# Hyena filters built in the opening of a fused hybrid diffusion step, ahead of the first adaLN sums

## The chip, the cores and the metric

One Trainium2 chip, of which the kernel uses one core. The metric is the device time of one launch in microseconds. Of a core's engines the text speaks of TensorE (PE; its weight loads are PEld), VectorE (DVE), ScalarE (ACT), GpSimd (POOL) and SyncE (SP, which here only issues transfers). Each engine runs its own instructions in the order in which the program gives them to it and waits on semaphores for the others.

## The reference, cut to what matters

One layer over two groups of 128 tokens (context and latent) with a model width of 2048. Each group is normed, scaled and shifted by adaLN columns, and goes through an input projection. One branch of the token mixer is a Hyena long convolution whose filters are made by a small sine network from 128 positions:

```python
z = concat([t, cos(w * f), sin(w * f)])            # 128 x 33
h = sin(fr[0] * (z @ w1 + b1))                      # 128 x 64
h = sin(fr[1] * (h @ w2 + b2))
h = (h @ w3 + b3).reshape(L, 2, HY_ORDER, D_HY)     # 2 directions, 2 orders, 1024 channels
h = h * exp(-t * abs(decay))
k = concat([h_fwd, 0, reversed(h_bwd[1:])])
k = k / (sum(abs(k)) + FILTER_EPS)
kf = rfft(k)                                        # used as uf * kf, and then y + u * bias
...
mod = silu(c) @ w_ada + b_ada                       # shift, scale, gate, twice: 6 x 2048
h = rmsnorm(x, g_pre) * (1 + scale) + shift
proj = h @ w_in
```

The filters depend on no token and on no adaLN value; they are needed when the first projected channels go through the convolution.

## The kernel before

All weights stream once from memory in pieces of 512 KB ("halves", 256 rows by 512 columns). A half of an ordinary weight is split on arrival: ACT rounds it to a high part `wh` (L223) and DVE takes the rest `wl` (L224), and PE runs three matmuls a tile (L288 to L290). So an ordinary half is 12 matmuls of 512 columns. A half of `w_ada` is not split; PE takes it as it is (L571, a few narrow matmuls), and after eight such halves one block of shift and scale columns is done.

`run_items` (L230) goes through a list of items, one for each half, and writes out the program in that order; what it decides is decided when the program is written, not on the chip. `feed_dma` (L205) issues the loads of halves on SP's queue, with at most `R` of them not yet taken up; `feed` (L214) writes out the splits of the halves that come up to `L` items ahead. `st` (L147) holds both; it starts with L=4 and R=16, and after the eighth `w_ada` half it is set to L=5, R=8.

Side work stands in a second list, `auxq`. `push` fills it, and after each item `pop_aux` (L166) takes pieces from it: in the opening ("free") one piece after each item, `idle(us)` holding the next one back for that much planned time. A piece's instructions stand in each engine's queue where it was taken.

The opening goes as follows. Small vectors come in on ACT's queue, the constants and the token tiles `x` on SP's. A transpose gives `cT` (Silu of the conditioning vectors) and bias columns. For each group ACT squares `x` (L386), `neg2_rstd` (L359) makes the norm's factor with a Sqrt, and `spread` (L377) turns it into a row `rb` by a matmul with ones. Then the items begin: eight `w_ada` halves (`mod_block(0, 2)`), with the transposed `x` (`x_block(0)`, L408) after the first; `to_cols` (L614) and `affine` (L629) make the first modulated block `hT`; then ordinary halves of `w_in` and `w_ada` halves alternate, one `w_in`, two `w_ada`, and so on, through six blocks.

The filters are side work in this stream. `mlp1` and `mlp2` (L450, L456) are the sine network with `sin_of` (L438); `filter_loads` (L419) puts the loads of the filters' weights on SP's queue; `filt_prep` (L461) splits the decay rates; `filt_h` (L470) makes one direction of one half of the channels of one order: two matmuls `pe` whose Exp ACT takes, one float32 matmul `ph`, which DVE multiplies by the Exp, and the absolute value on DVE; `filt_n` (L496) sums the absolute values on PE (`pn`) and makes diagonals; `filt_b` (L518) spreads them (`pi`); `filt_k` (L526) is the transform of the filter (`pc`, `pb`). There are four pairs of order and channel half, so eight `filt_h` and four of each other kind. The list `filt` (L539) and the last `push` (L1475) give their order, with pauses.

Of the kernel before, what the change touches and what calls it, by code (L numbers as in the profile page):

```python
# [11 lines left out]
F32 = mybir.dt.float32  # L12
# [5 lines left out]
P = 128  # L18
D = 2048
# [81 lines left out]
def hybrid_step(ctx: ExitStack, tc: tile.TileContext, ins, y_p, y_s, st_out):  # L101
# [18 lines left out]
    def s4(shape, dt=F32, n="s4"):  # L120
        return ar.tile(shape, dt, tag="s4", name=nm(n), bufs=NS4)
# [4 lines left out]
    def aux(shape=(P, W), n="aux"):  # L126
        return ps.tile(list(shape), F32, tag="ps", name=nm(n))
# [4 lines left out]
    def small(shape, n="sml", dt=F32):  # L132
        return sm_p.tile(shape, dt, name=nm(n))
# [13 lines left out]
    st = {"dma": 0, "split": 0, "used": 0, "out": 0, "L": 4, "R": 16, "bud": 0.0, "t": 0.0, "hold": 0.0, "free": True}  # L147
# [180 lines left out]
    for g in range(2):  # L328
        for h in range(2):
            xt[g][h] = s4([P, DH], n="x")  # L330
            SP.dma_start(out=xt[g][h], in_=xsrc[g][:, h * DH:(h + 1) * DH])
    lg = small([16, 1], "lg")
# [3 lines left out]
    pv = aux((P, 64), "pv")  # L336
    PE.transpose(pv, vr, ident[:64, :64])
    cT = cp.tile([P, KD, 34], F32, name="cT")
    V.memset(cT, 0.0)
    for g in range(2):  # L340
        A.activation(cT[:, :, 2 + g], pv[:, 16 * g:16 * g + 16], AF.Silu)
    gpre = cp.tile([P, 2, KD], F32, name="gpre")
    V.tensor_copy(gpre.rearrange("p a k -> p (a k)"), pv[:, 32:64])

    pb_ = aux((P, 96), "pbco")
    PE.transpose(pb_, bco, ident[:96, :96])
    bcol = cp.tile([P, 6, KD], F32, name="bcol")
    V.tensor_copy(bcol.rearrange("p a k -> p (a k)"), pb_)
    for i in (SCALE_M, SCALE_F):
        V.tensor_scalar(out=bcol[:, i, :], in0=bcol[:, i, :], scalar1=1.0, scalar2=None, op0=ALU.add)  # L350
# [32 lines left out]
    for g in range(2):  # L383
        ssx = small([P, 2], "ss0")
        for h in range(2):
            A.activation(s4([P, DH], n="junk"), xt[g][h], AF.Square, accum_out=ssx[:, h:h + 1])  # L386
        b0 = small([P, 1], "b0")
        V.tensor_scalar(out=b0, in0=ssx[:, 0:1], scalar1=1.0 / D, scalar2=RMS_EPS, op0=ALU.mult, op1=ALU.add)
        spread(g, diag_of(neg2_rstd(ssx[:, 1:2], b0)))

    def transpose_block(src, dst, col0, by=None):

        for kk2 in range(2):
            pt = aux((P, 2, 2, P), "pt")
            for a in range(2):
                for g in range(2):
                    kk = 2 * kk2 + a
                    x = src(g)[:, col0 + kk * P:col0 + (kk + 1) * P]
                    PE.transpose(pt[:, a, g, :], x, ident)  # L399
            o, i = dst[:, 2 * kk2:2 * kk2 + 2, :], pt.rearrange("p a g t -> p a (g t)")  # L400
            if by is None:
                A.copy(o, i)
            else:
                V.tensor_tensor(out=o, in0=i, in1=by.unsqueeze(1).broadcast_to([P, 2, 2 * P]), op=ALU.mult)

    xnT = [None] * NBLK

    def x_block(j):  # L408
        def f():
            xnT[j] = s4([P, 4, 2 * P], n="xnT")  # L410
            transpose_block(lambda g: xt[g][j // 2], xnT[j], (j % 2) * W, rb)
            if j == NBLK - 1:
                xt.clear()
        return piece(0.0, f, True)
# [4 lines left out]
    def filter_loads(o):  # L419
        def f():  # L420
            if o == 0:
                fl["tsel"], fl["dec"] = s4([8, 8 * P], n="tsel"), s2("dec")[:8, :]
                SP.dma_start(out=fl["tsel"], in_=ins["tsel"])
                SP.dma_start(out=fl["dec"], in_=ins["hy_decay"][0].rearrange("d o (c n) -> (d o c) n", n=W))
                SP.dma_start(out=dftm, in_=ins["cst"][:, DFT0:CST_W])
            for d in range(2):
                q = 2 * d + o
                t = s4([FH + 1, DH], n="w3")
                SP.dma_start(out=t[0:FH, :], in_=ins["hy_w3"][0][:, q * DH:(q + 1) * DH])
                SP.dma_start(out=t[FH:FH + 1, :], in_=ins["hy_b3"][:, q * DH:(q + 1) * DH])  # L430
                fl["w3", o, d] = t
# [29 lines left out]
    def filt_prep():  # L461
        dec = fl.pop("dec")
        dech, decl, tselr = s2("dech", F32R)[:8, :], s2("decl", F32R)[:8, :], s4([8, 8 * P], F32R, "tselr")
        V.scalar_tensor_tensor(out=dec, in0=dec, scalar=-1.0, in1=dec, op0=ALU.mult, op1=ALU.max)
        V.tensor_copy(dech, dec)
        V.tensor_tensor(out=decl, in0=dec, in1=dech.bitcast(F32), op=ALU.subtract)
        V.tensor_copy(tselr, fl.pop("tsel"))
        fl["exp"] = dech, decl, tselr

    def filt_h(o, hf, d):  # L470
        def f():
            q = d * 4 + o * 2 + hf
# [4 lines left out]
            e = s2("fe")
            A.activation(e, pe_, AF.Exp)
            ph = aux(n="ph")
            PE.matmul(ph, lhsT=h2fT, rhs=fl["w3", o, d][:, hf * W:hf * W + W], start=True, stop=True)  # L480
            V.tensor_tensor(out=e, in0=ph, in1=e, op=ALU.mult)
            if d == 1:
                V.memset(e[0:1, :], 0.0)
            ab = s2("fab")
            V.scalar_tensor_tensor(out=ab, in0=e, scalar=-1.0, in1=e, op0=ALU.mult, op1=ALU.max)
            fl[o, hf, d] = (e, ab)
            if d == 1:
                h0, ab0 = fl.pop((o, hf, 0))
                V.tensor_tensor(out=ab, in0=ab, in1=ab0, op=ALU.add)
                sd = s4([P, 2, W], n="fsd")  # L490
                V.tensor_tensor(out=sd[:, 0, :], in0=h0, in1=e, op=ALU.add)
                V.tensor_tensor(out=sd[:, 1, :], in0=h0, in1=e, op=ALU.subtract)
                fl[o, hf] = sd
# [32 lines left out]
    def filt_k(o, hf):  # L526
        def f():
# [7 lines left out]
            V.tensor_tensor(out=Kre[o][:, cs], in0=Kre[o][:, cs], in1=fl["hbias", o][:, cs], op=ALU.add)  # L535
# [3 lines left out]
    filt = [[], []]  # L539
    for o in range(2):  # L540
        for hf in range(2):
            filt[o] += [piece(1.4, filt_h(o, hf, 0), True), piece(3.2, filt_h(o, hf, 1), True), idle(3.0),
                     piece(0.8, filt_n(o, hf), True), idle(2.0), piece(0.0, filt_b(o, hf), True), idle(2.0),
                     piece(2.0, filt_k(o, hf), True)]
# [925 lines left out]
    for c in range(SPLIT, NPAIR):  # L1470
# [38 lines left out]
```

## Time and profile before

| | |
|---|---|
| median of 3 runs | 1639.32 us (1638.11 to 1642.18) |
| the profiled execution's own time | 1637.93 us |
| its span, first to last instruction | 1636.2 us |
| PE busy | 1586.4 us, 97% of the span |
| DVE, ACT busy | 1192.8 us, 729.5 us |
| read from memory | 384.03 MB, 239 GB/s over the span |

The span is what the trace shows; the device time of the same execution is 1.7 us more, and the median of the runs is 1.4 us above that. PE's busy time counts a pipelined matmul to its modelled end, so an engine that is busy throughout may still run at less than its best rate.

### The profile page before, as it was taken

To read this page: it belongs to the slowest core of one execution; us is meant where nothing else is said; L and a number is where in the kernel's file an instruction comes from. 1 tells how busy PE (TensorE), PEld (TensorE's weight loads), DVE (VectorE), ACT (ScalarE), POOL (GpSimd) and SP (SyncE) were. 2 spreads that over 40 slices of the span, in tenths; PEclk is the share of its full clock that TensorE was granted. 3 is DMA by queue.
4 is the path that set the end of the run, shared out by engine and by line. 5 is a ranking of instruction groups with operands and counts; after the bars stand their busy time and mean duration, and the time that the engine had idled before them with its cause. 6 is when DMAs were issued, how large, how long until landed. Compare 5 with 4: busy or idle time off the path is not lost.

```text
span 1636.2 us, 20371 instructions
## 1 busy us (share of the span) xinstructions
PE 1586.4 (97%) x7449; PEld 1248.3 (76%) x7449; DVE 1192.8 (73%) x1659; ACT 729.5 (45%) x946; POOL 70.0 (4%) x129
## 2 busy tenths in 40 slices
PE   4999999989999999999998999999999999999997
PEld 3665677657667788888887888888888888888886
DVE  3787877777774798778997665777878667778655
ACT  4533343333334455343545555455444354555532
POOL 0000021210011100000000000000000000000000
PEclk9999999999999999999999999999999999999999
DMA  9988898998778877786865765676678856666671
GB/s 328 336 279 309 291 301 255 334 294 284 231 270 272 276 236 246 241 286 215 285 205 211 231 172 176 208 214 194 203 259 269 293 180 195 203 210 211 208 238 53
DMA packets 208476, 396.88 MB, mean 243 GB/s; under 512 B 13220, under 2 KB 29919, under 8 KB 208376
## 3 DMA queue, kind: packets, MB, share of 16 engines
q1 hardware_dynamic: 201336, 373.88, 70.5%
q0 software_dynamic: 6800, 21.62, 4.4%
q8 instruction: 58, 0.95, 0.2%
q14 instruction: 42, 0.34, 0.1%
q10 hardware_dynamic: 240, 0.08, 0.0%
HBM read 384.03 MB, written 6.30 MB: 239 GB/s over the span
## 4 chain that ended last, share of the span: by engine, by line
PE 91%; DMA 4%; DVE 2%; ACT 1%; SPq 1%; issue 0%; ACTq 0%; DVEq 0%
PE acc L288 27%; PE acc L289 27%; PE acc L290 27%; PE ada L571 3%; DMA raw<-in_w_in_dram 2%; PE put L1353 1%; DMA raw<-in_w_ada_dram 1%; DVE wl L224 1%; SPq L210 1%; DMA raw<-in_ffn_w_up_dram 1%; PE ph L480 1%; ACT wh L223 0%; PE pt L399 0%; DMA vr<-in_norm_pre_mix_dram 0%; PE po L1031 0%
## 5 line engine op out<-in xcount | busy, mean ns | idle before, releaser
L224 DVE TENSOR_TENSOR wl<-raw,wh 128x1024 fp32r<-128x1024 f32 x504 | 596.1, 1220 | 195.8 <-ACT wh L223 188.2
L223 ACT CAST wh<-raw 128x1024 fp32r<-128x1024 f32 x504 | 502.9, 1048 | 175.9 <-PE acc L289 75.5
L288 PE MATMUL acc<-wh,hTh 128*128 128x512 f32 x704 | 284.2, 404 | 6.7 <-ACT wh L223 4.1
L289 PE MATMUL acc<-wl,hTh 128*128 128x512 f32 x704 | 276.8, 393 | 4.8 <-DVE wl L224 4.8
L288 PE MATMUL acc<-wh,h2Th 128*128 128x512 f32 x704 | 278.7, 396 | 2.8 <-ACT h2Th L1256 2.8
L290 PE MATMUL acc<-wh,hTl 128*128 128x512 f32 x704 | 276.5, 393 | 0.0
L290 PE MATMUL acc<-wh,h2Tl 128*128 128x512 f32 x704 | 275.4, 391 | 0.0
L289 PE MATMUL acc<-wl,h2Th 128*128 128x512 f32 x704 | 274.4, 390 | 0.0
L288 PEld LDWEIGHTS acc<-wh,hTh 128*128 128x128 f32 x704 | 133.4, 190 | 59.0 <-ACT wh L223 15.7
L600 DVE SCALAR_TENSOR_TENSOR adac<-raw,cT,adac 128x512 f32<-128x512 f32 x240 | 164.4, 746 | 0.0
L289 PEld LDWEIGHTS acc<-wl,hTh 128*128 128x128 f32 x704 | 133.4, 190 | 33.1 <-DVE wl L224 6.4
L290 PEld LDWEIGHTS acc<-wh,hTl 128*128 128x128 f32 x704 | 133.1, 189 | 28.9 <-DVE hTl L676 0.2
L288 PEld LDWEIGHTS acc<-wh,h2Th 128*128 128x128 f32 x704 | 132.7, 188 | 29.3 <-ACT h2Th L1256 3.2
L290 PEld LDWEIGHTS acc<-wh,h2Tl 128*128 128x128 f32 x704 | 132.5, 188 | 28.8 <-DVE h2Tl L1257 0.4
L289 PEld LDWEIGHTS acc<-wl,h2Th 128*128 128x128 f32 x704 | 132.7, 189 | 26.3
L288 PE MATMUL acc<-wh,actTh 128*128 128x512 f32 x352 | 137.3, 390 | 0.0
L290 PE MATMUL acc<-wh,actTl 128*128 128x512 f32 x352 | 137.1, 389 | 0.0
L289 PE MATMUL acc<-wl,actTh 128*128 128x512 f32 x352 | 137.0, 389 | 0.0
L1358 ACT ACTIVATE uv<-put,fcw 128x256 f32<-128x256 f32 x88 | 41.7, 475 | 91.6 <-DVE uv L1361 56.1
L1339 ACT COPY u<-acc 128x512 f32<-128x512 f32 x44 | 25.8, 587 | 116.8 <-PE acc L290 115.0
L290 PEld LDWEIGHTS acc<-wh,actTl 128*128 128x128 f32 x352 | 66.1, 188 | 13.8
L289 PEld LDWEIGHTS acc<-wl,actTh 128*128 128x128 f32 x352 | 66.1, 188 | 13.7
(311 smaller groups left out, 1594.9 us busy)
## 6 DMA issues: line engine op xcount, KB each, us to landing
raw<-in_w_ada_dram SPq DMA_DIRECT2D x192, 512.0 KB, 5.8
raw<-in_w_in_dram SPq DMA_DIRECT2D x176, 512.0 KB, 5.7
raw<-in_ffn_w_up_dram SPq DMA_DIRECT2D x176, 512.0 KB, 4.2
raw<-in_ffn_w_down_dram SPq DMA_DIRECT2D x88, 512.0 KB, 5.1
raw<-in_w_out_dram SPq DMA_DIRECT2D x32, 512.0 KB, 5.1
raw<-in_w_br_hy_dram SPq DMA_DIRECT2D x16, 512.0 KB, 4.7
raw<-in_w_br_ret_dram SPq DMA_DIRECT2D x16, 512.0 KB, 5.7
shw<-in_hy_short_w_dram POOLq DMA_DIRECT2D x18, 256.0 KB, 8.9
```

Of the source, the lines that this page charges most:

```text
L210: SP.dma_start(out=h.raw.rearrange("p a n -> p (a n)").rearrange("p (a n) -> p a n", a=per), in_=h.src)
L223: A.copy(h.hi, h.raw)
L224: V.tensor_tensor(out=h.lo, in0=h.raw, in1=h.hi.bitcast(F32), op=ALU.subtract)
L288: PE.matmul(self.ps[g], lhsT=h, rhs=wh, start=first, stop=False)
L289: PE.matmul(self.ps[g], lhsT=h, rhs=wl, start=False, stop=False)
L290: PE.matmul(self.ps[g], lhsT=l, rhs=wh, start=False, stop=last)
L480: PE.matmul(ph, lhsT=h2fT, rhs=fl["w3", o, d][:, hf * W:hf * W + W], start=True, stop=True)
L571: PE.matmul(z["ps"][32 * t:32 * t + 32, :nt * P], lhsT=cT[:, kb + kk, 2 - 2 * i:34 - 2 * i], rhs=w[:, kk, :], start=i == 0 and kb + kk < 4 ...
L600: V.scalar_tensor_tensor(out=t, in0=w, scalar=c, in1=t if kt else bias, op0=ALU.mult, op1=ALU.add)
L1339: A.copy(u[:, g, :], ch.ps[g])
L1353: PE.transpose(pt[:, a, g, :], u[:, g, kk * P:(kk + 1) * P], ident)
L1358: A.activation(o, i, AF.Copy, scale=fcw[:, 1, col:col + 1])
```

## The change

The filters' loads go to the front of SP's queue, between the constants and the token tiles (`filter_loads(0)`, `x_load(0)`, `filter_loads(1)`, `x_load(1)`). The sine network, the Exp factors of all four pairs and three of the four `filt_h` are written out before the first item, around the squares and the norms. `filt_h` now does both directions in one piece, and its absolute value is on ACT. The other pieces come one after each item from the first on, without pauses. The biases are loaded later and on POOL's queue (`bias_load`), and added to `Kre` in one go (`bias_add`). The look-ahead starts with L=0, so that no `w_in` half is split before the eighth `w_ada` half is taken, and R=10.

```diff
-    st = {..., "L": 4, "R": 16, ...}
+    st = {..., "L": 0, "R": 10, ...}
...
+    filter_loads(0)
+    x_load(0)
+    filter_loads(1)
+    x_load(1)
     cT = cp.tile([P, KD, 34], F32, name="cT")
...
+    mlp1()
     gpre = cp.tile([P, 2, KD], F32, name="gpre")
...
+    filt_prep()
+    mlp2()
+    filt_e(0, 0)
+    filt_e(0, 1)
+    squares(0)
+    filt_h(0, 0)()
+    filt_e(1, 0)
+    filt_e(1, 1)
+    squares(1)
+    filt_h(0, 1)()
+    for g in range(2):
+        input_norm(g)
+    filt_h(1, 0)()
...
+    def filt_e(o, hf):
+        dech, decl, tselr = fl["exp"]
+        e = s4([P, 2, W], n="fe")
+        for d in range(2):
+            q = d * 4 + o * 2 + hf
+            pe_ = aux(n="pe")
+            PE.matmul(pe_, lhsT=tselr[:, q * P:(q + 1) * P], rhs=dech, start=True, stop=False)
+            PE.matmul(pe_, lhsT=tselr[:, q * P:(q + 1) * P], rhs=decl, start=False, stop=True)
+            A.activation(e[:, d, :], pe_, AF.Exp)
+        fl["e", o, hf] = e
+    def filt_h(o, hf):
+        def f():
+            e = fl.pop(("e", o, hf))
+            for d in range(2):
+                ph = aux(n="ph")
+                PE.matmul(ph, lhsT=h2fT, rhs=fl["w3", o, d][:, hf * W:hf * W + W], start=True, stop=True)
+                V.tensor_tensor(out=e[:, d, :], in0=ph, in1=e[:, d, :], op=ALU.mult)
+            V.memset(e[0:1, 1, :], 0.0)
+            ab, sd = s4([P, 2, W], n="fab"), s4([P, 2, W], n="fsd")
+            A.activation(ab, e, AF.Abs)
+            V.tensor_tensor(out=sd[:, 0, :], in0=e[:, 0, :], in1=e[:, 1, :], op=ALU.add)
+            V.tensor_tensor(out=sd[:, 1, :], in0=e[:, 0, :], in1=e[:, 1, :], op=ALU.subtract)
...
     def filt_n(o, hf):
         def f():
+            ab = fl.pop(("ab", o, hf))
+            V.tensor_tensor(out=ab[:, 0, :], in0=ab[:, 0, :], in1=ab[:, 1, :], op=ALU.add)
...
-            t = s4([P, DH], n="hbias")
-            SP.dma_start(out=t, in_=ins["hy_bias"][0][o].partition_broadcast(P))
+            G.dma_start(out=t, in_=ins["hy_bias"][0][o].partition_broadcast(P))
...
-    push(x_block(0), idle(3.2), mlp[0], x_block(1), idle(3.0), mlp[1], idle(2.0), piece(0.0, filter_loads(0)), x_block(2), x_block(3),
-         idle(10.0), piece(2.0, filt_prep), *filt[0], piece(0.0, filter_loads(1)), piece(0.0, filt_done(0)), idle(14.0),
-         *filt[1], piece(0.0, filt_done(1)), piece(2.0, ret_gamma),
+    push(N(0, 0), x_block(0), piece(1.0, filt_h(1, 1), True), B(0, 0), N(0, 1), K(0, 0), B(0, 1), N(1, 0), x_block(1),
+         K(0, 1), B(1, 0), N(1, 1), K(1, 0), B(1, 1), x_block(2), K(1, 1), piece(0.0, filt_done), x_block(3),
+         idle(8.0), piece(0.0, bias_load), idle(30.0), piece(2.0, ret_gamma),
          idle(4.0), piece(2.0, ret_powers), idle(4.0), piece(2.0, ret_tables), idle(6.0), piece(0.1, ret_cols, True),
+         piece(2.4, bias_add))
```

## Rows read from the trace of the kernel before

**Rows 1.** The page, busy time: engine, us, share of the span, instructions.
```profile
PE 1586.4 (97%) x7449; PEld 1248.3 (76%) x7449; DVE 1192.8 (73%) x1659; ACT 729.5 (45%) x946; POOL 70.0 (4%) x129
```

**Rows 2.** Engines by stretch: length, busy us, granted clock (PEclk), DMA share, GB/s.
```profile
8.00:16.00 8.00, 1.49 (x4) 0.86 (x4) 2.30 (x13) 5.55 (x12) 0.00 (x0) 1.00 1.05 349
30.00:34.00 4.00, 4.00 (x12) 2.89 (x11) 1.61 (x2) 1.24 (x2) 0.00 (x0) 0.66 1.09 362
180.00:200.00 20.00, 20.00 (x96) 13.56 (x96) 17.00 (x62) 5.25 (x5) 0.68 (x2) 1.00 1.01 353
```

**Rows 3.** Timeline of the opening: start, duration, engine and line, what ended its wait.
```profile
8.71 1.06 ACT L386 ACTIVATE junk<-x 128x1024 f32<-128x1024 f32 x1
...
9.26 0.25 DVE L350 TENSOR_SCALAR bcol<-bcol 128x16 f32<-128x16 f32 x2
...
10.91 1.28 ACT L362 ACT_TABLE_LOAD   x1
12.21 0.29 ACT L362 ACTIVATE nt<-ss,b 128x1 f32<-128x1 f32 x1
...
14.36 0.27 ACT L381 COPY rb<-prb 128x128 f32<-128x128 f32 x1 [1.86 <-PE prb L380]
...
19.79 1.97 PE L399 MATMUL pt<-cst,x 128*128 128x128 f32 x8
...
21.69 3.58 PE L571 MATMUL ada<-raw,cT 128*32 128x256 f32 x56
...
25.30 1.04 ACT L223 CAST wh<-raw 128x1024 fp32r<-128x1024 f32 x1 [6.15 <-DMA raw<-in_w_in_dram]
26.25 0.36 ACT L575 COPY adap<-ada 128x256 f32<-128x256 f32 x1
26.37 1.22 DVE L224 TENSOR_TENSOR wl<-raw,wh 128x1024 fp32r<-128x1024 f32 x1 [3.88 <-ACT wh L223]
...
29.04 0.62 ACT L674 CAST hTh<-xnT 128x512 fp32r<-128x512 f32 x1
...
29.71 0.79 PE L288 MATMUL acc<-wh,hTh 128*128 128x512 f32 x1 [2.61 <-ACT hTh L674]
...
34.04 0.43 PE L452 MATMUL p<-cst,hyw 33*64 33x128 f32 x2
...
34.97 1.09 PE L399 MATMUL pt<-cst,x 128*128 128x128 f32 x8
...
36.66 0.31 ACT L446 ACTIVATE h1T<-arg 64x128 f32<-64x128 f32 x1 [0.61 <-DVE arg L445]
```

**Rows 4.** The chain that ended last, 60 to 115 us: start, us, what.
```profile
62.78 0.60 DVE dec L464
...
65.19 0.50 PE pe L475
...
65.92 1.06 PE ph L480 x2
66.97 0.57 PE ada L571 x8
...
70.25 0.23 PE acc L289
...
73.34 0.98 PE pn L501 x8
...
77.89 0.86 PE pi L521 x2
...
82.70 0.86 PE pc L531 x2
```

**Rows 5.** Groups of instructions, 30 to 200 us: count, busy us, mean ns of one.
```profile
L481 DVE TENSOR_TENSOR fe<-ph,fe 128x512 f32<-128x512 f32 x8 | 5.5, 687 | 1.8 <-PE ph L480 1.8
L478 ACT ACTIVATE fe<-pe 128x512 f32<-128x512 f32 x8 | 4.8, 598 | 18.3 <-PE pe L476 18.3
...
L483 DVE MEMSET fe<- 1x512 f32 x4 | 1.9, 485 | 0.6 <-DVE fe L481 0.6
```

More of the change, by code (lines that the diff above doesn't have):

```diff
@@ L146, in hybrid_step @@
     halves, items = [], []
-    st = {"dma": 0, "split": 0, "used": 0, "out": 0, "L": 4, "R": 16, "bud": 0.0, "t": 0.0, "hold": 0.0, "free": True}
+    st = {"dma": 0, "split": 0, "used": 0, "out": 0, "L": 0, "R": 10, "bud": 0.0, "t": 0.0, "hold": 0.0, "free": True}
     def depth(look, raw):
@@ L327, in hybrid_step, with x_load @@
     xsrc = [ins["x_prompt"][0], ins["x_sample"][0]]
-    for g in range(2):
+    def x_load(g):
         for h in range(2):
@@ L333, in hybrid_step @@
     G.dma_start(out=lg, in_=ins["ret_decay_logit"][0].rearrange("d (h o) -> (d h) o", o=1))
[L336 to L350, printed above, removed]
     ones = cp.tile([P, P], F32, name="ones")
@@ L381, in spread, with squares, input_norm @@
         A.copy(rb[:, g * P:(g + 1) * P], pr)
-    for g in range(2):
-        ssx = small([P, 2], "ss0")
+    ssx0 = [small([P, 2], "ss0") for _ in range(2)]
+    def squares(g):
         for h in range(2):
-            A.activation(s4([P, DH], n="junk"), xt[g][h], AF.Square, accum_out=ssx[:, h:h + 1])
+            A.activation(s4([P, DH], n="junk"), xt[g][h], AF.Square, accum_out=ssx0[g][:, h:h + 1])
+    def input_norm(g):
         b0 = small([P, 1], "b0")
-        V.tensor_scalar(out=b0, in0=ssx[:, 0:1], scalar1=1.0 / D, scalar2=RMS_EPS, op0=ALU.mult, op1=ALU.add)
-        spread(g, diag_of(neg2_rstd(ssx[:, 1:2], b0)))
@@ L391, in transpose_block @@
[L391 to L414, printed above, removed]
+        V.tensor_scalar(out=b0, in0=ssx0[g][:, 0:1], scalar1=1.0 / D, scalar2=RMS_EPS, op0=ALU.mult, op1=ALU.add)
+        spread(g, diag_of(neg2_rstd(ssx0[g][:, 1:2], b0)))
     fl, Kre, KB = {}, {}, {}
     def filter_loads(o):
[L420 to L431, printed above, removed]
@@ new lines, in filter_loads @@
+        if o == 0:
+            fl["tsel"], fl["dec"] = s4([8, 8 * P], n="tsel"), s2("dec")[:8, :]
+            SP.dma_start(out=fl["tsel"], in_=ins["tsel"])
+            SP.dma_start(out=fl["dec"], in_=ins["hy_decay"][0].rearrange("d o (c n) -> (d o c) n", n=W))
+        for d in range(2):
+            q = 2 * d + o
+            t = s4([FH + 1, DH], n="w3")
+            SP.dma_start(out=t[0:FH, :], in_=ins["hy_w3"][0][:, q * DH:(q + 1) * DH])
+            SP.dma_start(out=t[FH:FH + 1, :], in_=ins["hy_b3"][:, q * DH:(q + 1) * DH])
+            fl["w3", o, d] = t
@@ L432, in f, with bias_load @@
+        if o == 0:
+            SP.dma_start(out=dftm, in_=ins["cst"][:, DFT0:CST_W])
+        Kre[o], KB[o] = s4([P, DH], n="Kre"), s4([P, DH], n="KB")
+    def bias_load():
+        for o in range(2):
             t = s4([P, DH], n="hbias")
-            SP.dma_start(out=t, in_=ins["hy_bias"][0][o].partition_broadcast(P))
+            G.dma_start(out=t, in_=ins["hy_bias"][0][o].partition_broadcast(P))
             fl["hbias", o] = t
-            Kre[o], KB[o] = s4([P, DH], n="Kre"), s4([P, DH], n="KB")
@@ L436, in filter_loads, with bias_add @@
-        return f
+    def bias_add():
+        for o in range(2):
+            V.tensor_tensor(out=Kre[o], in0=Kre[o], in1=fl.pop(("hbias", o)), op=ALU.add)
     def sin_of(dst, ps, b, fr):
@@ L462, in filt_prep @@
         dec = fl.pop("dec")
-        dech, decl, tselr = s2("dech", F32R)[:8, :], s2("decl", F32R)[:8, :], s4([8, 8 * P], F32R, "tselr")
+        both, tselr = s4([8, 2, W], F32R, "dech"), s4([8, 8 * P], F32R, "tselr")
+        dech, decl = both[:, 0, :], both[:, 1, :]
         V.scalar_tensor_tensor(out=dec, in0=dec, scalar=-1.0, in1=dec, op0=ALU.mult, op1=ALU.max)
@@ L468, in filt_prep @@
         fl["exp"] = dech, decl, tselr
-    def filt_h(o, hf, d):
-        def f():
+    def filt_e(o, hf):
+        dech, decl, tselr = fl["exp"]
+        e = s4([P, 2, W], n="fe")
+        for d in range(2):
             q = d * 4 + o * 2 + hf
-            dech, decl, tselr = fl["exp"]
             pe_ = aux(n="pe")
@@ L476, in f @@
             PE.matmul(pe_, lhsT=tselr[:, q * P:(q + 1) * P], rhs=decl, start=False, stop=True)
[L477 to L493, printed above, removed]
+            A.activation(e[:, d, :], pe_, AF.Exp)
[3 more added lines that the diff above has]
+            e = fl.pop(("e", o, hf))
+            for d in range(2):
+                ph = aux(n="ph")
[6 more added lines that the diff above has]
+            V.tensor_tensor(out=sd[:, 1, :], in0=e[:, 0, :], in1=e[:, 1, :], op=ALU.subtract)
+            fl[o, hf] = sd
+            fl["ab", o, hf] = ab
         return f
@@ L497, in f @@
         def f():
-            ab = fl.pop((o, hf, 1))[1]
+            ab = fl.pop(("ab", o, hf))
+            V.tensor_tensor(out=ab[:, 0, :], in0=ab[:, 0, :], in1=ab[:, 1, :], op=ALU.add)
             pn = aux((P, 4), n="pn")
             for c in range(4):
-                PE.matmul(pn[:, c:c + 1], lhsT=ab[:, c * P:(c + 1) * P], rhs=ones[:, 0:1], start=True, stop=True)
+                PE.matmul(pn[:, c:c + 1], lhsT=ab[:, 0, c * P:(c + 1) * P], rhs=ones[:, 0:1], start=True, stop=True)
             inv, dg = small([P, 4], "finv"), s2("fdg")
@@ L509, in filt_n, with filt_done @@
         return f
-    def filt_done(o):
-        def f():
+    def filt_done():
+        for o in range(2):
             for d in range(2):
                 fl.pop(("w3", o, d))
-            fl.pop(("hbias", o))
-        return f
     def filt_b(o, hf):
@@ L534, in f @@
             PE.matmul(pb, lhsT=k("S"), rhs=sd[:, 1, :], start=True, stop=True)
-            V.tensor_tensor(out=Kre[o][:, cs], in0=Kre[o][:, cs], in1=fl["hbias", o][:, cs], op=ALU.add)
             V.tensor_tensor(out=KB[o][:, cs], in0=pb, in1=inv, op=ALU.mult)
         return f
[L539 to L544, printed above, removed]
+    filter_loads(0)
@@ new lines, in hybrid_step @@
+    x_load(0)
+    filter_loads(1)
+    x_load(1)
+    cT = cp.tile([P, KD, 34], F32, name="cT")
+    V.memset(cT, 0.0)
+    pv = aux((P, 64), "pv")
+    PE.transpose(pv, vr, ident[:64, :64])
+    for g in range(2):
+        A.activation(cT[:, :, 2 + g], pv[:, 16 * g:16 * g + 16], AF.Silu)
+    mlp1()
+    gpre = cp.tile([P, 2, KD], F32, name="gpre")
+    V.tensor_copy(gpre.rearrange("p a k -> p (a k)"), pv[:, 32:64])
+    pb_ = aux((P, 96), "pbco")
+    PE.transpose(pb_, bco, ident[:96, :96])
@@ new lines, in hybrid_step, with transpose_block @@
+    bcol = cp.tile([P, 6, KD], F32, name="bcol")
+    V.tensor_copy(bcol.rearrange("p a k -> p (a k)"), pb_)
+    for i in (SCALE_M, SCALE_F):
+        V.tensor_scalar(out=bcol[:, i, :], in0=bcol[:, i, :], scalar1=1.0, scalar2=None, op0=ALU.add)
+    filt_prep()
[8 more added lines that the diff above has]
+    filt_h(0, 1)()
+    for g in range(2):
+        input_norm(g)
+    filt_h(1, 0)()
+    def transpose_block(src, dst, col0, by=None):
+        for kk2 in range(2):
+            pt = aux((P, 2, 2, P), "pt")
+            for a in range(2):
+                for g in range(2):
+                    kk = 2 * kk2 + a
+                    x = src(g)[:, col0 + kk * P:col0 + (kk + 1) * P]
+                    PE.transpose(pt[:, a, g, :], x, ident)
+            o, i = dst[:, 2 * kk2:2 * kk2 + 2, :], pt.rearrange("p a g t -> p a (g t)")
+            if by is None:
+                A.copy(o, i)
+            else:
+                V.tensor_tensor(out=o, in0=i, in1=by.unsqueeze(1).broadcast_to([P, 2, 2 * P]), op=ALU.mult)
@@ L546, in hi_lo, with x_block, f @@
+    xnT = [None] * NBLK
+    def x_block(j):
+        def f():
+            xnT[j] = s4([P, 4, 2 * P], n="xnT")
+            transpose_block(lambda g: xt[g][j // 2], xnT[j], (j % 2) * W, rb)
+            if j == NBLK - 1:
+                xt.clear()
+        return piece(0.0, f, True)
     def hi_lo(val, n):
@@ L1472, in hybrid_step @@
     down_half(SPLIT, NPAIR, down_second, True)
-    mlp = [piece(0.5, mlp1, True), piece(0.5, mlp2, True)]
-    push(x_block(0), idle(3.2), mlp[0], x_block(1), idle(3.0), mlp[1], idle(2.0), piece(0.0, filter_loads(0)), x_block(2), x_block(3),
-         idle(10.0), piece(2.0, filt_prep), *filt[0], piece(0.0, filter_loads(1)), piece(0.0, filt_done(0)), idle(14.0),
-         *filt[1], piece(0.0, filt_done(1)), piece(2.0, ret_gamma),
-         idle(4.0), piece(2.0, ret_powers), idle(4.0), piece(2.0, ret_tables), idle(6.0), piece(0.1, ret_cols, True))
+    N = lambda o, hf: piece(0.4, filt_n(o, hf), True)
+    B = lambda o, hf: piece(0.0, filt_b(o, hf), True)
+    K = lambda o, hf: piece(2.0, filt_k(o, hf), True)
+    push(N(0, 0), x_block(0), piece(1.0, filt_h(1, 1), True), B(0, 0), N(0, 1), K(0, 0), B(0, 1), N(1, 0), x_block(1),
+         K(0, 1), B(1, 0), N(1, 1), K(1, 0), B(1, 1), x_block(2), K(1, 1), piece(0.0, filt_done), x_block(3),
+         idle(8.0), piece(0.0, bias_load), idle(30.0), piece(2.0, ret_gamma),
+         idle(4.0), piece(2.0, ret_powers), idle(4.0), piece(2.0, ret_tables), idle(6.0), piece(0.1, ret_cols, True),
+         piece(2.4, bias_add))
     run_items()
```

## The prediction

> **What bounds the kernel now.** I read the page first: PE is busy for 97% of the span [rows 1], and by the engines' busy time by stretch it is so from the first weights on, 4.00 of 4.00 us at 30 us, 20.00 of 20.00 at 180 [rows 2]. So behind the opening nothing but PE's own work sets the pace, and work taken off PE there comes back whole. The transfers are not far behind: 353 to 362 GB/s in the same stretches, a share of 1.01 to 1.09 of the sixteen transfer engines [rows 2]. Ahead of 30 us it is otherwise: between 8 and 16 us PE has 1.49 us of work, ACT 5.55 of 8, and the transfers run at 1.05 [rows 2].
>
> The timeline of the opening says what that time waits for [rows 3]. The norm factors are done early (first `rb` at 14.36 us). PE then takes the `w_ada` halves as they land, the last of them at 21.69 + 3.58 = 25.3 us. From there a chain of small steps leads to the first main matmul at 29.71: ACT copies the sums only at 26.25, because it stood in the split of the first `w_in` half, for which it had waited 6.15 us; then the columns, the modulation, the rounding of `hT` (29.04 + 0.62 = 29.66). The opening is bound by transfers, and PE, DVE and ACT have room in it. Call T the time of that first main matmul: now 29.7. As PE is never short of work behind it in this stretch, the change is worth (work taken from PE behind T) minus (how much later T comes).
>
> **What is taken from PE behind T.** One `filt_h` lasts from 65.19 to the next piece at 66.97, 1.78 us, for the two `pe` and one `ph` [rows 4]; eight are 14.2. All of them lie ahead of the new T. One piece is taken after each of the first eight items, so N(0,0), N(0,1), N(1,0), B(0,0), B(0,1) and K(0,0) lie ahead of it too: 3 x 0.98 for `pn`, 2 x 0.86 for `pi`, and `pc` and `pb` at 0.86 each [rows 4], 6.4 us. The two matmul pairs of the sine network are 0.43 each [rows 3], 0.9. Together 21.5. Where a `pn` does not follow narrow matmuls it is cheaper, and some of each 1.78 is the switch between shapes, so I take 20.5. `x_block(0)` lay ahead of T and still does. N(1,1), B(1,0), B(1,1) and three K stay behind T.
>
> **How much later T comes.** The loads set ahead of the `w_ada` halves are 0.03 + 0.02 + 0.26 + 4 x 0.27 = 1.4 MB; at 362 GB/s [rows 2] 3.8 us, so the last `w_ada` half lands near 29. I expect nothing to wait for it, since the engines are later. Each engine goes through its queue in order, so I follow the new order with the durations of before.
>
> *First stretch, ACT.* Silu is done when the first square starts now, at 8.71 [rows 3]; its vectors come on ACT's own queue and don't move. A round of the sine network takes from `p` at 34.04 to the end of Sin at 36.97, 2.9 us [rows 3], so the first ends at 11.5. DVE then has the bias columns (four small instructions, two of them 0.25 us [rows 3]; I take 0.6) and `filt_prep`, which stands from 62.78 to the `pe` at 65.19, 2.4 us [rows 4]; both stand in its queue ahead of the second round: 14.5. The second round is 2.5 us without its matmul, and a table load of 1.28 [rows 3] comes before the Exp: 18.3. From here ACT has no gap: eight Exp of 0.60 [rows 5] are 4.8, the squares of a group take from 8.71 to 10.91, 2.2, twice [rows 3], two absolute values of 128x1024 are priced at the 1.05 of a square, and a table load of 1.28 for Sqrt. Sum 12.6, so Sqrt starts at 31. One norm takes from 12.21 to 14.63, 2.4 us [rows 3], and the second starts on ACT only when `rb` of the first is copied: 4.8. `rb` is complete at 35.8, where it was complete near 19 before. PE and DVE work of `filt_h(0,0)` and `filt_h(0,1)` is hidden under this ACT stretch.
>
> *Second stretch, PE and DVE by turns.* `filt_h(1,0)` stands on PE behind the second norm's matmul and ahead of the first `w_ada` matmul, so no adaLN work starts before 36. Then: two `ph` (2.1), DVE's last product (0.69), the memset of one row (0.49 [rows 5]), sum and difference and the sum of absolute values (3 x 0.69): 5.4 us until `pn` can start, since DVE has N's addition behind them. `pn` 0.9; two w_ada items (0.57 each) around `x_block(0)` (1.09 [rows 3]); two `ph` of `filt_h(1,1)` 2.1; again 0.69 + 0.49 + 3 x 0.69 = 3.3 of DVE before N(0,1)'s `pn`; 0.9; then item 6, `pc`, `pb`, item 7, `pi`, item 8: 3 x 0.57 + 3 x 0.86 = 4.3. Sum 19.1, which ends the eighth `w_ada` item at 54.9.
>
> *Third stretch, no split ahead.* From the copy of the sums to `hT` took 26.25 to 29.66, 3.4 us, of which 0.4 was DVE's `wl` in the way [rows 3]: 3.0 now. Before, the first `w_in` half was split by then. Now two splits are written behind `hT`: `wh` 1.04, and `wl` twice 1.22 [rows 3] on DVE. N(1,0)'s addition (0.69) stands behind both on DVE, and its `pn` (0.9) stands ahead of the first main matmul on PE. That is 5.1 us in which before there were 0.05. T = 54.9 + 3.0 + 5.1 = 63.0.
>
> *PE's clock.* After PE's pause ahead of 29.71 the granted clock was 0.66 on average between 30 and 34 us [rows 2], so the lower level of 1.2 GHz stood for most of it; the same eight transposes took 1.97 us at 19.79 and 1.09 at 34.97 [rows 3]. In the new opening PE pauses at 24 to 33 us for the norms, and again and again for DVE. PE's matmuls between `rb` and T are about 14 us at the full rate. None at the low level adds 0, all of them 14. PE is at work for two thirds of that time, which is nearer to the run of `w_ada` matmuls that went at full rate than to the pause: I take a quarter, 3.5. T = 66.5.
>
> The Trainium skill (TensorE: Matmul & The Clock Gate, "What's actually happening") says that the array's clock is halved by default and that activity releases it. Rows 2 agree as far as they go, with 0.66 behind a pause and 1.00 under load; by that rule taken strictly every pause in the new opening would be paid again, and the sum would go towards 77.
>
> The Trainium skill (ScalarE: Activation LUTs, "What ACT_TABLE_LOAD costs") puts a switch of function set at 1283 ns and a drain of about 1380 ns. The load here takes that 1.28, and the Sqrt behind it started 0.02 us later [rows 3], so no drain shows; by the page's figure the Exp and Sqrt switches would make T an estimated 2.8 us later.
>
> *The rest.* The bias loads move from SP's queue to POOL's, which has no work at 30 us and 0.68 of 20 us at 180 [rows 2]; hidden under PE, and 1.0 MB of 353 GB/s, 3 us, if the transfers were the bound. The absolute values leave DVE and the bias is added in two passes; no gain, as PE was not waiting for DVE behind 30 us. SP's queue has ten loads out in the opening, not sixteen; they have landed long before T.
>
> **Sum.** T later by 66.5 - 29.7 = 36.8, PE work less by 20.5: +16.3. On the profiled execution's 1637.9 that is 1654.2; the median lies 1.4 above it, so I say 1655. What lies behind the sixth block is written out as before, and I move it as a whole.
>
> **Rivals.**
> (a) *The opening hides it: faster.* If ACT's and DVE's steps overlap the `w_ada` loads as PE's do, T stays bound by transfers: 29.7 + 3.8, and 20.5 come back: 1639.3 - 16.7 = 1623. For it: transfers at 1.05, PE mostly idle until 16 us [rows 2]. Against it: the steps are in line on ACT up to 36 us by rows of this kernel, and the `w_ada` matmuls stand behind them on PE. It decides where T is below 29.7 + 20.5 = 50.2. Chance 0.06.
> (b) *The gap closes by half.* T near 50: 1639, no difference. That needs some 14 us of my second and third stretch to lie side by side. Chance 0.05.
> (c) *The transfers become the bound behind T.* A `w_in` and a `w_ada` half take PE 12 x 0.23 + 0.57 = 3.3 us [rows 4], and 1.05 MB in 3.3 us are 318 GB/s, against 353 to 362 that the rows show [rows 2]. The pieces that slowed PE there are gone, and transfers stand still for some 25 us in the opening. If the loads then run short by a few per cent over the 180 us of alternating halves, PE waits 5 to 10 us more: 1663. Against it: ten halves lie ready at T, and at 180 to 200 us PE had 20.00 of 20.00 at 353 GB/s. Chance 0.10.
> (d) My forecast, T between 60 and 74, 1648 to 1663: 0.79.
>
> **Numbers.** 1655, range 1646 to 1668: it reaches down to a T of 57, and up to all of the low clock (T at 77) or to (c). 0.3% of 1639 is 5 us, about what a measurement tells from no change: faster 0.06, the same 0.05, slower 0.89.
>
> **What would show it.** In the profile after: the first main matmul (L288's line, `acc<-wh,hTh`) near 66 us; ACT without a gap from 18 to 31 us; `rb` copied at 36; PE waiting for DVE's `fab` ahead of `pn`; the transfers' rate falling to little around 35 us; PE full again behind T, and the later stages all moved by the same 16 us. I am wrong if the first main matmul comes before 50 us, if PE waits for loads behind T, or if the later stages don't move as one.

## The result, and the profile after

| | before | after |
|---|---|---|
| median of 4 runs each | 1640.61 us (1638.11 to 1642.18) | 1659.41 us (1658.24 to 1661.47) |
| ratio, 95% interval | | 1.0123 (1.0110 to 1.0136) |
| the profiled execution's own time | 1637.93 us | 1661.47 us |
| its span | 1636.2 us | 1659.7 us |
| T, the first main matmul | 29.71 us | 73.08 us |

The change costs 18.8 us where 16.3 were forecast, and the time lies in the range. The profiled execution of before was faster than all four of its runs, and that of after was the slowest of its own, so the two traces lie 23.5 us apart, not 18.8. By the traces T came 43.4 us later, and 43.4 - 23.5 = 19.9 us came back behind it; by the medians it would be 24.6.

The page of after, busy time, against [rows 1]: PE has as many instructions as before and is busy 19.5 us longer.

```profile
PE 1605.9 (97%) x7449; PEld 1257.9 (76%) x7449; DVE 1187.7 (72%) x1649; ACT 734.7 (44%) x949; POOL 71.0 (4%) x131
```

Engines by stretch, after (columns as in [rows 2]):

```profile
30.00:34.00 4.00, 0.85 (x3) 0.58 (x3) 1.94 (x10) 0.97 (x4) 0.00 (x0) 1.00 1.08 361
11.00:23.00 12.00, 11.89 (x21) 6.58 (x22) 5.04 (x13) 8.64 (x16) 0.00 (x0) 1.00 1.05 270
42.00:62.00 20.00, 20.00 (x81) 8.74 (x81) 8.63 (x22) 1.64 (x2) 0.00 (x0) 1.00 0.61 192
...
66.00:73.00 7.00, 1.65 (x8) 1.65 (x8) 4.08 (x6) 3.21 (x5) 0.00 (x0) 0.74 0.00 0
...
180.00:200.00 20.00, 20.00 (x105) 13.85 (x104) 15.00 (x24) 7.47 (x11) 0.00 (x0) 1.00 1.00 303
```

Three things stand here. At 30 us, where PE had 4.00 of 4.00 before, it has 0.85. From 42 to 62 us it is busy throughout, though by the forecast the eighth `w_ada` item would have ended at 54.9. From 66 to 73 us PE has 1.65 us of work, DVE 4.08 and ACT 3.21, and there is no transfer at all: no more than ten halves may be out, and they have landed.

The timeline of the first stretch, after:

```profile
5.05 0.34 PE L516 MATMUL pv<-cst,vr 64*128 64x64 f32 x1 [5.05 <-DMA vr<-in_norm_pre_ffn_dram]
...
13.45 1.28 ACT L448 ACT_TABLE_LOAD   x1
...
14.74 2.07 ACT L448 ACTIVATE fe<-pe 128x512 f32<-128x512 f32 x4
...
20.08 1.06 ACT L460 ACTIVATE fab<-fe 128x1024 f32<-128x1024 f32 x1 [1.21 <-DVE fe L458]
...
27.50 1.06 ACT L460 ACTIVATE fab<-fe 128x1024 f32<-128x1024 f32 x1 [2.35 <-DVE fe L458]
...
34.75 0.27 ACT L365 COPY rb<-prb 128x128 f32<-128x128 f32 x1 [1.85 <-PE prb L364]
```

And of the second and third:

```profile
38.06 1.08 PE L593 MATMUL ada<-raw,cT 128*32 128x256 f32 x8
...
41.58 1.84 PE L473 MATMUL pn<-ones,fab 128*128 128x1 f32 x8 [2.44 <-DVE fab L470]
...
47.27 3.78 PE L456 MATMUL ph<-w,h2fT 65*128 65x512 f32 x4
...
51.99 2.08 PE L491 MATMUL pi<-fdg,ones 128*128 128x512 f32 x2
...
61.53 1.08 PE L593 MATMUL ada<-raw,cT 128*32 128x256 f32 x8
...
62.54 1.12 PE L491 MATMUL pi<-fdg,ones 128*128 128x512 f32 x2
...
63.60 0.64 PE L593 MATMUL ada<-raw,cT 128*32 128x256 f32 x8
...
66.73 0.62 ACT L696 CAST hTh<-xnT 128x512 fp32r<-128x512 f32 x1
67.26 1.99 ACT L223 CAST wh<-raw 128x1024 fp32r<-128x1024 f32 x2
...
68.33 2.36 DVE L224 TENSOR_TENSOR wl<-raw,wh 128x1024 fp32r<-128x1024 f32 x2 [0.25 <-ACT wh L223]
70.61 0.69 DVE L470 TENSOR_TENSOR fab<-fab 128x512 f32<-128x512 f32 x1
71.35 1.87 PE L473 MATMUL pn<-ones,fab 128*128 128x1 f32 x8 [6.18 <-DVE fab L470]
...
73.08 0.77 PE L288 MATMUL acc<-wh,hTh 128*128 128x512 f32 x1
```

The reader should compare like with like here: eight `ada` matmuls take 1.08 us at 61.53 and 0.64 at 63.60; two `pi` take 2.08 at 51.99 and 1.12 at 62.54. So PE was at 1.2 GHz up to about 62.5 us and at 2.4 behind it. The granted-clock column shows 1.00 for the whole of that time, with no sign of the rise; only the durations tell.

How much came back, and where, is read from matmuls that both programs have in the same order. The 461st main matmul, behind the last filter piece of before, and a run of `w_ada` matmuls far behind, each first of before, then of after:

```profile
198.21 0.39 PE L289 MATMUL acc<-wl,hTh 128*128 128x512 f32 x1
```

```profile
222.35 0.39 PE L289 MATMUL acc<-wl,hTh 128*128 128x512 f32 x1
```

```profile
428.56 1.92 PE L571 MATMUL ada<-raw,cT 128*32 128x512 f32 x16
```

```profile
451.53 1.93 PE L593 MATMUL ada<-raw,cT 128*32 128x512 f32 x16
```

They come 24.14 and 22.97 us later. So 19.2 of the 43.4 us came back by 198 us, where the filters lie in the kernel before, and the rest moved nearly as one: compared one by one from there to the end, the main matmuls are 21.4 to 25.8 us later, the last of them 23.4.

### The profile page after: what moved, and what is told of

Read it like the earlier page. It is cut to its first block, busy times and chain, and to the rows that moved or that the text cites. A ratio compares the mean times of both kernels' runs of the same rounds, so it can differ in the third digit from the quotient of the medians.

```text
span 1659.7 us, 20366 instructions
## 1 busy us (share of the span) xinstructions
PE 1605.9 (97%) x7449; PEld 1257.9 (76%) x7449; DVE 1187.7 (72%) x1649; ACT 734.7 (44%) x949; POOL 71.0 (4%) x131
## 4 chain that ended last, share of the span: by engine, by line
PE 91%; DVE 4%; DMA 2%; ACT 1%; issue 1%; SPq 0%; DVEq 0%; ACTq 0%
PE acc L288 27%; PE acc L289 26%; PE acc L290 26%; PE ada L593 3%; DMA raw<-in_w_ada_dram 1%; PE put L1375 1%; DVE wl L224 1%; PE ph L456 1%; DMA raw<-in_ffn_w_up_dram 0%; PE pt L551 0%; PE pn L473 0%; ACT wh L223 0%; DMA sh<-x 0%; PE pt L1267 0%; PE pi L491 0%
## 5 line engine op out<-in xcount | busy, mean ns | idle before, releaser
L290 PEld LDWEIGHTS acc<-wh,hTl 128*128 128x128 f32 x704 | 133.6, 190 | 29.2 <-DVE pw L932 0.4
L1361 ACT COPY u<-acc 128x512 f32<-128x512 f32 x44 | 25.8, 587 | 118.5 <-PE acc L290 116.7
```

The source lines that it names most:

```text
L290: PE.matmul(self.ps[g], lhsT=l, rhs=wh, start=False, stop=last)
L1361: A.copy(u[:, g, :], ch.ps[g])
```

## The experiments

The theory: T sets the loss, and T is so late because the filter pieces run in line with the norms, at PE's low clock, with unsplit weights at the end. The rivals: the loads ahead of the tokens are to blame; or the missing split is. Medians of before, measured beside them, were 1639.68 us (16 runs) for the first four kernels and 1640.23 us (21 runs) for the last three.

**1. The missing split alone.** In the kernel before:

```diff
-    st = {..., "L": 4, "R": 16, ...}
+    st = {..., "L": 0, "R": 10, ...}
```

> The kernel before with the start of the look-ahead alone changed (L=0, R=10). Line theory (the loss is T, the first main matmul, pushed out by filter steps that stand in line on ACT, DVE and PE ahead of the first adaLN sums): the copy of the sums no longer waits for a split, about 1 us earlier, and the first split now lies behind hT, about 2 us later: T 30 to 32, +0 to +2 us, 1640 to 1643. Rival (the missing split ahead is what costs): T near 40, +8 us or more.

Measured: 1641.4 us, ratio 1.0006 (0.9992 to 1.0021). T did not move, as the timeline shows:

```profile
29.53 0.80 PE L288 MATMUL acc<-wh,hTh 128*128 128x512 f32 x1 [3.19 <-ACT wh L223]
```

PE now waits 3.19 us for `wh` instead of 2.61 for `hTh` [rows 3]. What pays for that is the sums' copy, which no longer stands behind a split:

```profile
25.48 0.37 ACT L575 COPY adap<-ada 128x256 f32<-128x256 f32 x1 [6.22 <-PE ada L571]
```

It starts at 25.48 instead of 26.25. So the missing split does not move T: from `hTh` complete (28.54) to the first main matmul it is 1.0 us here, against 5.7 in the changed kernel, where another piece's DVE work stands behind the splits. Right behind T a little is paid. PE waits another 0.46 us for `wl` and stays at the low clock to about 36 us (before to about 33), and the next half starts 2.0 us later than before (at 36.56 there):

```profile
38.52 0.50 PE L288 MATMUL acc<-wh,hTh 128*128 128x512 f32 x1
```

Whether the whole run gets longer by that is not settled, since the interval of the ratio has 1 in it.

**2. The loads alone.** The kernel before, with the filters' loads ahead of the token tiles and all else in its place:

```diff
     for g in range(2):
+        filter_loads(g)
...
-    def filter_loads(o):
+    def bias_loads(o):
```

> The kernel before with the filters' loads alone moved ahead of the token tiles, their biases staying where they were and all filter work staying side work of the stream. Line theory: the opening of the kernel before is bound by transfers, 1.4 MB at some 360 GB/s push T by up to 3.8 us to 31 to 34; +1 to +4 us, 1641 to 1645. Rival (the loads ahead of the w_ada halves cause the loss): T beyond 40, +10 us or more.

Measured: 1649.34 us, ratio 1.0051 (1.0033 to 1.0070). The timeline of PE and, ahead of it, the first square on ACT:

```profile
14.23 1.06 ACT L404 ACTIVATE junk<-x 128x1024 f32<-128x1024 f32 x1 [8.30 <-DMA x<-in_x_prompt_dram]
```

```profile
25.67 1.08 PE L575 MATMUL ada<-raw,cT 128*32 128x256 f32 x8
...
32.76 0.64 PE L575 MATMUL ada<-raw,cT 128*32 128x256 f32 x8 [0.55 <-DMA raw<-in_w_ada_dram]
...
40.02 0.80 PE L288 MATMUL acc<-wh,hTh 128*128 128x512 f32 x1 [2.61 <-ACT hTh L678]
```

T is 10.3 us later, not 3.8, and the time is above the 1641 to 1645 that were expected. The same stretch as in [rows 2] moves 236 GB/s instead of 349, at almost the same share:

```profile
8.00:16.00 8.00, 0.00 (x0) 0.00 (x0) 0.15 (x1) 1.15 (x2) 0.00 (x0) 1.00 0.95 236
```

So the loads have a price of their own, 8 to 10 us by the ratio, the medians and T. In the changed kernel it is not paid: there the first `ada` matmul starts at 38.06, and no `ada` of the opening waits for `w_ada`.

**3. The pieces behind the adaLN sums.** The changed kernel, with `x_block(0)` first and a pause that holds the other pieces back until the eight `w_ada` halves are taken:

```diff
-    push(N(0, 0), x_block(0), piece(1.0, filt_h(1, 1), True), B(0, 0), N(0, 1), K(0, 0), B(0, 1), N(1, 0), x_block(1),
+    push(x_block(0), idle(4.0), N(0, 0), piece(1.0, filt_h(1, 1), True), B(0, 0), N(0, 1), K(0, 0), B(0, 1), N(1, 0), x_block(1),
```

> The changed kernel, with only the transposed x between the first eight w_ada items; the seven filter pieces that stood there follow behind the eighth. Line theory: T falls from 73 by these pieces at their low-clock price and their waits, to 56 to 61, and 8 us of PE work come back behind T at the full rate: 1648 to 1654. Rival (these pieces fill time in which PE waits for loads or norms anyway): T stays within 3 us of 73 and the time rises to 1662 to 1668.

Measured: 1652.99 us, ratio 1.0078 (1.0055 to 1.0101). The timeline of PE:

```profile
37.97 1.08 PE L593 MATMUL ada<-raw,cT 128*32 128x256 f32 x8
...
40.89 3.34 PE L593 MATMUL ada<-raw,cT 128*32 128x256 f32 x56
...
48.36 0.79 PE L288 MATMUL acc<-wh,hTh 128*128 128x512 f32 x1 [3.19 <-ACT wh L223]
...
82.72 1.84 PE L473 MATMUL pn<-ones,fab 128*128 128x1 f32 x8 [3.57 <-DVE fab L470]
84.49 1.08 PE L593 MATMUL ada<-raw,cT 128*32 128x256 f32 x8
```

T falls by 24.7 us, further than expected (48.4 us where 56 to 61 were), but the span only by 9.0, to 1650.7, so 15.7 us are lost again behind T, where 8 were expected. Behind T lie now the seven pieces (some 8 us: three `pn`, two `pi`, `pc`, `pb` and the four `ph` passes, by [rows 4]), a wait of 3.57, and behind that wait a stretch at the low clock (`ada` at 1.08 again) that lasts from the wait to about 89 us, 7 us and so worth about 3.5: by this estimate some 15 of the 15.7. The pieces ahead of T are thus no pure loss, and behind this wait for a piece's DVE work the clock was low again. This run also divides the 43.4 us: 24.7 belong to the seven pieces and their low clock, and 18.6, what T is still late by, to the first stretch.

**4. PE kept at work.** The changed kernel, with 68 matmuls of 512 columns added in the pauses (their results are not used; one copy on ACT makes their operand): 4 behind the sine network, 20 ahead of the norms, 5 inside them, 10, 5 and 24 ahead of the `pn` of N(0,0), N(0,1) and N(1,0):

```diff
+    def warm(n):
...
+        pw = aux(n="warmps")
+        for _ in range(n):
+            PE.matmul(pw, lhsT=onesr, rhs=wr[:, 0, :], start=True, stop=True)
...
+    warm(4)
...
+    warm(20)
...
+        warm(0 if g else 5)
...
+            if (o, hf) != (1, 1):
+                warm({(0, 0): 10, (0, 1): 5, (1, 0): 24}[o, hf])
```

> The changed kernel with added matmuls (128x128 by 128x512, results not used) where PE paused in the opening: 4 ahead of the Exp factors' matmuls, 20 and 5 ahead of the two norms' matmuls, 10, 5 and 24 ahead of the first three sums of absolute values, and one copy on ACT for their operand. Line theory with the low clock as the term that was too small: PE leaves the low level well before 62 us, a pair of ph takes 2.1 us in place of 3.6, T falls from 73 to 63 to 67, the time to 1649 to 1655. Rival (DVE and ACT alone set T, and PE's rate there is hidden): T stays at 72 to 76, the time at 1659 to 1664.

Measured: 1650.48 us, ratio 1.0057 (1.0031 to 1.0082). The copy of `rb` on ACT, and the timeline of PE:

```profile
36.09 0.27 ACT L365 COPY rb<-prb 128x128 f32<-128x128 f32 x1 [1.54 <-PE prb L364]
```

```profile
26.11 7.73 PE L530 MATMUL warmps<-warm,onesr 128*128 128x512 f32 x20
...
37.71 0.64 PE L608 MATMUL ada<-raw,cT 128*32 128x256 f32 x8
...
46.83 1.13 PE L493 MATMUL pi<-fdg,ones 128*128 128x512 f32 x2
...
54.84 0.64 PE L608 MATMUL ada<-raw,cT 128*32 128x256 f32 x8
...
63.53 0.47 PE L288 MATMUL acc<-wh,hTh 128*128 128x512 f32 x1
```

With 68 matmuls more, T is 9.6 us earlier and the median 8.9 us less. `ada` takes 0.64 from the first item on, `pi` 1.13: the high level. From `rb` complete (36.4) to the end of the eighth `w_ada` item (55.48) are 19.1 us, as forecast for that stretch, though the added matmuls stand in it; in the changed kernel it was 29.2. The clock was the difference.

**5. Only what the opening has room for.** The kernel before; `tsel` and the decay rates loaded first, `filt_prep` and the four `pe` pairs of order 0 ahead of the norms, their Exp behind the norms:

```diff
+    filt_prep()
+    early = [(0, hf, d) for hf in range(2) for d in range(2)]
+    pes = {w: pe_of(*w) for w in early}
...
+    for w in early:
+        t = s4([P, 2, W], n="fe")[:, 0, :]
+        A.activation(t, pes.pop(w), AF.Exp)
+        fl["e", w] = t
```

> The kernel before, with as much of the filters in the opening as stands in nobody's way: the two small loads (decay rates, selector) ahead of the token tiles, filt_prep on DVE and the four pairs of pe matmuls of the first order ahead of the norms, their four Exp on ACT behind the norms; all else stays side work of the stream. Line theory: nothing of it stands ahead of the adaLN sums for longer than their weights take to land, so T stays at 29.5 to 31 and 4 x 0.72 = 2.9 us of PE work come back: -1 to -3.5 us, 1636 to 1639. Rival (any filter work ahead of the sums pushes them out, as in the changed kernel): T at 34 or more, 1642 or more.

Measured: 1635.36 us, ratio 0.9973 (0.9958 to 0.9987), faster than both kernels. The timeline:

```profile
9.14 0.79 PE L400 MATMUL pe<-dech,tselr 8*128 8x512 f32 x1 [3.43 <-DVE b L412]
...
19.78 2.06 ACT L417 ACTIVATE fe<-pe 128x512 f32<-128x512 f32 x4
...
29.84 0.55 PE L288 MATMUL acc<-wh,hTh 128*128 128x512 f32 x1 [2.61 <-ACT hTh L687]
```

T stays (29.84), and the span falls by 3.0 us, to 1633.2. A `pe` pair took 65.92 - 65.19 = 0.73 us behind T [rows 4]; four are 2.9. The main matmul that stood at 198.21 comes 2.2 us earlier, and the medians lie 4.9 apart, with 2.1 to 6.9 by the interval. So work taken from PE behind T does come back where T doesn't pay for it; that it is the whole 2.9 agrees with these numbers, but they do not settle it to a microsecond.

**6. Which of the loads.** Experiment 2, with `tsel`, the decay rates and the `b3` rows left at their old places, so that the weights `w3` (four of 64 rows, 256 KB each) and the transform's table stand ahead:

```diff
     for g in range(2):
+        filter_loads(g)
...
-    def filter_loads(o):
+    def bias_loads(o):
...
-                t = s4([FH + 1, DH], n="w3")
-                SP.dma_start(out=t[0:FH, :], in_=ins["hy_w3"][0][:, q * DH:(q + 1) * DH])
-                SP.dma_start(out=t[FH:FH + 1, :], in_=ins["hy_b3"][:, q * DH:(q + 1) * DH])
-                fl["w3", o, d] = t
+                SP.dma_start(out=fl["w3", o, d][FH:FH + 1, :], in_=ins["hy_b3"][:, q * DH:(q + 1) * DH])
```

> The kernel with the loads alone moved, but with the four one-row loads of 4 KB and the two loads of 8 rows left where the kernel before had them; the four loads of 64 rows (256 KB) and the transform's table stay ahead of the token tiles. There the loads cost 10 us of T in place of the 3.8 that their bytes would take. If the few-row loads are the slow ones, T falls from 40 to 33 or 34 and the time to 1641 to 1644. If the loads of 64 rows are, T stays at 38 to 40 and the time at 1646 to 1650.

Measured: 1646.34 us, ratio 1.0037 (1.0024 to 1.0049). T at 36.45, 6.7 later where experiment 2 had 10.3. By stretch:

```profile
8.00:16.00 8.00, 0.00 (x0) 0.00 (x0) 1.07 (x7) 3.38 (x5) 0.00 (x0) 1.00 0.97 249
```

The result lies between the two expectations: by difference, two thirds of the delay belong to the large loads, 1.3 MB in 6.7 us or some 195 GB/s, and one third to loads that together are less than 0.1 MB. Of those, `tsel` and the decay rates stood ahead of the token tiles in experiment 5 too, and T did not move there; so the third lies with the four `b3` rows of 4 KB, or with small and large loads together. What makes the large ones slow (their 64 rows are the obvious difference to the tiles') was not measured by itself.

**7. The third stretch.** The changed kernel with the split ahead given back and N(1,0) one item later:

```diff
-    st = {..., "L": 0, "R": 10, ...}
+    st = {..., "L": 4, "R": 16, ...}
...
-    push(N(0, 0), x_block(0), piece(1.0, filt_h(1, 1), True), B(0, 0), N(0, 1), K(0, 0), B(0, 1), N(1, 0), x_block(1),
+    push(N(0, 0), x_block(0), piece(1.0, filt_h(1, 1), True), B(0, 0), N(0, 1), K(0, 0), B(0, 1), x_block(1), N(1, 0),
```

> The changed kernel with the look-ahead of the kernel before at the start (L=4, R=16), so that the first split lies ahead of hT again, and with N(1,0) one item later, behind the first main matmuls. Line theory, third stretch: hT to the first main matmul falls from 5.7 us to under 0.5, T from 73 to 67 to 70 (the split adds 1.2 us of DVE ahead), 0.9 to 1.7 us of pn come back behind T: 1654 to 1657. Rival (the end of the opening is set elsewhere): T and time as in the changed kernel, 1658 to 1661.

Measured: 1656.52 us, ratio 1.0101 (1.0075 to 1.0128). The timeline:

```profile
67.19 0.62 ACT L696 CAST hTh<-xnT 128x512 fp32r<-128x512 f32 x1
...
67.86 0.50 PE L288 MATMUL acc<-wh,hTh 128*128 128x512 f32 x1 [1.37 <-ACT hTh L696]
```

The first main matmul follows 0.05 us behind `hTh`, as before the change, and T is 5.2 us earlier. The 461st main matmul is 5.3 us earlier too (217.03 for 222.35), but the medians differ by 2.9 us (ratios 1.0123 and 1.0101, whose intervals overlap), so what of the 5.2 is kept at the end is not settled.

The run does not isolate the third stretch, as the second went otherwise. Its length is the same, 29.3 us from `rb` to the eighth `w_ada` item for 29.2, but its course is not (timeline, and engines from 56 to 62 us):

```profile
47.64 2.48 PE L456 MATMUL ph<-w,h2fT 65*128 65x512 f32 x4
...
50.05 0.64 PE L593 MATMUL ada<-raw,cT 128*32 128x256 f32 x8
...
55.92 1.87 PE L473 MATMUL pn<-ones,fab 128*128 128x1 f32 x8 [3.60 <-DVE fab L470]
```

```profile
56.00:62.00 6.00, 6.00 (x20) 3.08 (x20) 1.90 (x7) 0.00 (x0) 0.00 (x0) 0.50 0.00 0
```

On the same matmuls in the same order as in the changed kernel, the clock rose within `ph` (2.48 us for 3.78), at about 48.7 us and so some 14 us earlier than there. Then the split now written ahead stood on DVE in front of N(0,1)'s addition, PE waited 3.60 us, and from 56 to 62 us it was at the low level again, at 6.00 of 6.00 us busy. What the earlier rise gave, the split and the wait took.

## Why the prediction was right, and where it was off

*The model held.* That 43.4 less 19.9 makes the 23.5 of the two spans is no test of it, as the 19.9 is their difference. The test is where it came back: 19.2 (forecast 20.5) by the main matmul at 198.21 us, among the filters' pieces, and little behind. Experiment 5 shows this half alone, in small, and experiment 4 that a T 9.6 us earlier brings the median down by 8.9.

*The step that was off is "I take a quarter, 3.5", the clock.* Without it the forecast of T was 63.0; the trace has 73.1. First stretch 0.8 us early (`rb` at 35.0 for 35.8), second 29.2 for 19.1, third 3.0 and 5.7 for 3.0 and 5.1. So the whole second stretch went at 1.2 GHz until its last two matmul groups, and the price was about 10, between the quarter taken and "all of them 14". Experiment 4 took 9.6 of it away. The step reasoned that PE at work for two thirds of the time is nearer to load than to pause. But PE counted as busy 11.89 of 12.00 and 20.00 of 20.00 us and stayed at 1.2 GHz, so being busy on the profile's count wasn't enough here. Nor is the 10 us a fixed price: in experiment 7 the clock rose some 14 us earlier on the same matmuls. The Trainium skill (TensorE: Matmul & The Clock Gate, "What's actually happening") says that the array is throttled by default and that activity releases it; the default is what the trace shows from the start to 62.5 us. The "towards 77" that the prediction set beside it was nearer to 73.1 than its own 66.5.

*The first stretch was right by two errors.* "ACT without a gap" was wrong: it waited 1.21 and 2.35 us for DVE's product, which waited for `ph` at the low clock (1.9 us a direction, half of the 3.78 for `ph` x4, where [rows 4] have 1.06). But the opening began some 3 us earlier: `pv` at 5.05 us, Silu done by 5.7 instead of 8.71. (The first round's end in the sum, 11.5, should read 11.6.) "Its vectors come on ACT's own queue and don't move" was wrong too. The Trainium skill (ScalarE: Activation LUTs, "What ACT_TABLE_LOAD costs") adds a drain to a change of function set; the Exp at 14.74 starts 0.01 us behind its table load, so this trace shows none either.

*"3.8 us" for the loads* should have been about 10 (experiment 2), but rightly nothing waited for them, as the engines came later still.

*The third stretch* was right in size, 5.7 for 5.1. Experiment 7 took 5.2 off T, but with the second stretch altered as well.

*"The transfers' rate falling to little around 35 us"* was wrong: 361 GB/s at 30 to 34. The pause came at 66 to 73 us, at 0 GB/s, when the ten halves were all there. Rival (c) did not come: at 180 to 200 us PE has 20.00 of 20.00 at 303 GB/s, and the view of waits from 74 to 200 us has one row for PE, for a split:

```profile
PE acc L289 <- DVE wl L224: 1.6, 1, 1.6
```

*Against the medians* the loss was forecast only 2.5 us low (16.3 for 18.8), where by the traces it was 7.2 low (16.3 for 23.5). That the medians came out nearer is luck: the profiled execution of after was 2.1 us above its median and that of before 2.7 below its own.

## What to carry to other kernels

An opening that waits for transfers has room only for work whose inputs are already there and that stands in no queue ahead of what the first main matmul needs: move that work alone (experiment 5), and for the rest count how much later the first main matmul comes. Work that PE does by turns with DVE should be priced at the low clock first, with the high one as the other end of the range, since a busy PE on the page does not say that the clock has risen; the duration of one known matmul does. And loads moved to the front of a queue are priced by a row of such loads, not by the best rate of large ones.

## What was not expected of the hardware

- PE was busy without a break from 42 to 62 us, and nearly so from 11 to 23, with the `pe`, `ph`, narrow `ada`, `pn`, `pi`, `pc` and `pb` matmuls, and stayed at 1.2 GHz. In experiment 7 the same matmuls in the same order had the rise within the `ph` at 47.64. In experiment 4 it came within a run of 20 matmuls of 128x512 that began at 26.11, and in experiment 3 about 0.3 us into 56 `ada` matmuls in line that began at 40.89, so soon that the work ahead of them may have brought it. Which property of the matmuls decides, or whether it is the moment at which they come, was not separated.
- Transfers with a share of 0.95 to 0.97 of the sixteen engines moved 236 to 249 GB/s (experiments 2 and 6), where a share of 1.05 stood for 349 before [rows 2]: the share says how long the engines are taken, not what they move.
- The small vectors on ACT's queue landed 3 us earlier in the changed kernel, where the token tiles no longer stood at the front of SP's queue. The transpose of them started at 8.19 before, at 5.05 there, at 5.01 in experiment 5 with only `tsel` and the decay rates in front of the tiles, and at 6.88 in experiment 6 with the large loads in front.
